# Score products for the GQA maxima: 72 rows of the array instead of 64

## The chip, the cores and the metric

The kernel runs on one core of a Trainium2 chip. The metric is device time in microseconds, the median of several runs. The core's engines each work through their own queue in order and wait for one another on semaphores: TensorE (PE, with its weight loads listed apart as PEld), VectorE (DVE), ScalarE (ACT), GpSimd (POOL), and SyncE (SP), which issues the weight stream's DMAs.

## The reference

One step of a two-layer backbone, float32. The 128 prompt tokens and 512 sample tokens go through the same layers; the sample's attention also reads a cache of 128 keys. Cut to what the change touches:

```python
def gqa_attend(q, k, v):                       # 8 query heads, 2 key heads, 64 features
    q5 = q.reshape(b, t, GQA_KV_HEADS, GQA_GROUP, HEAD_DIM)
    def blk(qb):
        s = jnp.einsum('bqkgd,bskd->bkgqs', qb, k).astype(jnp.float32) * scale
        p = jax.nn.softmax(s, axis=-1).astype(v.dtype)
        return jnp.einsum('bkgqs,bskd->bqkgd', p, v)
...
h = rms_norm(x, norm1_g) * (1 + sc1) + sh1
z = h @ w_in                                   # GQA q, k, v | gated convolution | differential q, k, v
... # per-head norms, rotary, o_g = gqa_attend, o_c = convolution, o_d = differential attention
x = x + g1 * (jnp.concatenate([o_g, o_c, o_d], axis=-1) @ w_out)
h = rms_norm(x, norm2_g) * (1 + sc2) + sh2
a, u = jnp.split(h @ ffn_up, 2, axis=-1)
x = x + g2 * ((jax.nn.silu(dwconv3(a, ffn_conv_w, ffn_conv_b)) * u) @ ffn_down)
```

The softmax of the sample runs over 640 keys (512 latent, 128 cached), that of the prompt over its own 128.

## The kernel before, in words

Tokens lie in five tiles of 128: tile 0 is the prompt, 1 to 4 the sample; the attention takes them in the order 1, 2, 3, 4, 0. Every large product is made in three passes of a reduced float32 type, from values split into a high and a low part: high by high, low by high, high by low. A layer runs through projections, attention, output projection and a gated MLP.

The part at issue is the GQA attention. Its operands stand with features on the partitions:

- `KG` holds a key head's high parts twice (rows 0 to 63 and 64 to 127), `KL` its low parts (rows 0 to 63) and ones in rows 64 to 71.
- `qTg` holds a tile's queries, high parts in rows 0 to 63 and low parts in 64 to 127; `qTm` holds the high parts again in rows 0 to 63, and in rows 64 to 71 the maxima that are to be taken off. Each has two places in turn (`s_q`, L1476), so a tile's queries are stacked, transposed on PE and evacuated while the tile before is at work (`q_tasks`, L1481; for the first two tiles `q_trans` and `q_evac`, L1341 and L1350).

First come scores with queries on the rows, made only for their maxima (`scores`, L1551). For each of the 8 heads `u` and each half of the keys (320 columns; 128 for the prompt) there are two products into one bank of the pair `p`:

```python
PE.matmul(o, q[:, u, :], KG[:, a_, c0:c0 + w], start=True, stop=False)
PE.matmul(o, q[0:64, u, :], KL[0:64, a_, c0:c0 + w], start=False, stop=True)
```

The queries are the weights. The first gives high by high and low by high over 128 rows, the second high by low over 64. DVE reduces the pair's 640 columns to one maximum (`maxima`, L1570). Four maxima are split, transposed on PE (`mm`) and written into rows 64 to 71 of `qTm` by DVE or ACT (`m_v`, `m_s`, L1604), each head's in its own row and zeros in the others. Then come the scores by key (`c_mm`, L1623), where keys are the weights: one product of KG with `qTg` over 128 rows and one of KL with `qTm` over 72 rows, whose ones add the negative maximum. ACT takes the exponential, PE multiplies by the values (`VG`, 64 weight columns), and POOL or DVE adds up the exponentials for the sums (`acc`). The differential attention beside it uses `KD` with 96 rows, into the same pairs `p`, and its exponentials `P` are transposed and multiplied by `VD`.

The order is set in two steps before anything runs. `Schedule` (L573) orders the attention's tasks by estimated times, places and a priority; a place such as one of `qTm`'s two (`Buf`) is free again when the stated number of readers has run. `Graph` (L181) then takes down every instruction with what it reads and writes, and emits them in the order of the best of 15 list plans made from estimated costs. All instructions bear the line of that helper, L316, in the profile, so they are told apart by their tiles.

Of the kernel before, what the change touches and what calls it, by code (L numbers as in the profile page):

```python
# [65 lines left out]
# us from the end of an instruction to the start of one that waits for it  # L66
# [8 lines left out]
class View:  # L75
    # A part of a tile that is made when its first instruction is emitted; `idx` holds the element numbers in a partition.
# [104 lines left out]
class Graph:  # L181
    # Takes down the instructions of the program in its order, with what each reads and writes, and emits them in an
    # order that keeps the engines busy: of the instructions whose inputs are there, the one that can wait least.
# [6 lines left out]
    # ---- pools and tiles  # L190
# [37 lines left out]
    def _places(self):  # L228
        # a tile's first instructions come after all of the tile's whose place it takes, and after its pool's opening
        for p in self.all:  # L230
            for n, row in p.tags.values():
                place = [None] * n
                for t in sorted((t for t in row if t.first is not None), key=lambda t: t.first.n):
                    i = min(range(n), key=lambda i: -1 if place[i] is None else place[i].ops[-1].n)
                    t.old, place[i] = place[i], t
                    t.kw = {**t.kw, "tag": f"{t.kw['tag']}_{i}", "bufs": 1}
        # pools that lie where closed ones lay come after them
        for p in self.pools:
            p.base = p.below.base + p.below.size if p.below else 0
            lo, hi = p.base, p.base + p.size  # L240
            if p.side == "right":
                top = SB_TOP if p.kind == "sb" else 16384
                lo, hi = top - hi, top - lo
            p.lo, p.hi = lo, hi
            p.under = [q for q in p.earlier if q.lo < hi and lo < q.hi]
            p.opened.before.update(q.shut for q in p.under)
        for p in self.all:
            for t in p.tiles:
                own = set(t.ops)
                for op in t.ops:  # L250
                    if op is t.first or not (op.deps & own):
                        op.before.add(p.opened)
                        if t.old is not None:
                            op.deps.update(t.old.ops)
                        for q in p.under:
                            op.deps.update(q.ops)
# [14 lines left out]
    # ---- instructions  # L271
# [58 lines left out]
    # ---- order  # L330
# [29 lines left out]
    def deadlines(self):  # L360
        """Priorities: the latest starts of the plan made from the end."""
# [5 lines left out]
        free = deque()  # L367
# [52 lines left out]
    def plan(self):  # L420
# [3 lines left out]
        later = {k: [] for k in now}       # (when the inputs are there, number, op)  # L424
        ready = {k: [] for k in now}       # (priority, number, when, op)
# [24 lines left out]
        while True:  # L450
# [24 lines left out]
            if op.extra:  # L475
                # bytes that the queues carry one after another
                e = self.queue(busy, now[k] + (2.6 if k == "G" else 1.2), op.extra) + 0.95
# [7 lines left out]
    def queue(self, busy, t, n):  # L485
        """Takes the first free time from t on among the busy ones (kept in order), returns its end."""
# [14 lines left out]
def cost(key, name, args, kw, outs, ins):  # L501
    """Estimated us on the engine, and on the DMA queues."""
# [37 lines left out]
class Slots:  # L540
    # interchangeable places; `free` holds when each can be taken again, None while it is held
    # with `line` the takers are served in order of urgency
# [9 lines left out]
class Buf:  # L552
    # a place held from the task that fills it to the last of `reads` readers
# [10 lines left out]
class Task:  # L564
    # alts: (engine, estimated us, emit); takes: buffers it fills first; reads: buffers it is done with
# [7 lines left out]
class Schedule:  # L573
    # Orders tasks for the engines' queues: whichever can start first, the more urgent one among near equals.
# [56 lines left out]
def tile_hybrid_prefix_dit_step(  # L631
# [38 lines left out]
    # banks b0..b3; beside them c0..c3, which the attention takes as the pairs p0 and p1  # L670
# [17 lines left out]
    def f32(t):  # L688
        return t.bitcast(F32)

# [5 lines left out]
    # sel[p, h] = 1 where p % 4 == h  # L696
    sel = T(P0, [128, 4], "sel")
    V.tensor_reduce(out=sel, in_=ident.rearrange("p (j h) -> p h j", h=4), axis=AX.X, op=ALU.add)
    # pick[:, r, q] = 1 where q == r
# [4 lines left out]
    # sum4[p, r] = 1 where p % 32 == r  # L704
# [19 lines left out]
    # silu(c) channel-major, zero-padded to 32 columns  # L724
# [8 lines left out]
    # vectors of a layer, channels on the partitions  # L733
# [87 lines left out]
    def mod_vec(l, v, k, raw):  # L821
        # the products of both conditions added up on DVE, then summed over the partitions
# [17 lines left out]
    def mod_quarter(q, v, g, raw):  # L840
        # the first two vectors in quarters of the channels; each 32 rows of the sums hold every fourth block of rows
# [55 lines left out]
    # order of the 128-row blocks of w_out: the convolution's first  # L897
# [114 lines left out]
    def tok_gemm(ah, al, nks, evac, tail=0, order=None, post=None, off=OFF, banks=ACC, tiles=range(NT)):  # L1012
        # the `tail` last units go tile by tile, the others block by block
# [35 lines left out]
    def chan_gemm(units, evacs, hh, hl):  # L1049
        # units: the banks of both halves of the columns; the first halves of all units come before the second ones  # L1050
# [11 lines left out]
    class Norm:  # L1062
# [8 lines left out]
        def sq(self, t, half):  # L1071
            # mean of squares of half the channels, with the guard in the first half's
# [34 lines left out]
        def mod(self, t, part, src=None):  # L1107
            # a quarter of the channels in place, or half of them from `src`
# [49 lines left out]
    def rope(z, t, H, d, key, tmp):  # L1158
        # z = z * cos * g + rot(z * g) * sin in place, [128, H, d]
# [14 lines left out]
    def rsqrt(ms):  # L1174
        # ms: [128, n] -> ms ** -0.5 in a new tile
# [17 lines left out]
    # ======================= layers =======================  # L1193
# [25 lines left out]
    for l in range(DEPTH):  # L1219
        a, b = (sides if l % 2 else sides[::-1])   # b: hT, mixa, attention, f; a: mixc, kv, prj, h2T  # L1220
# [22 lines left out]
        # keys, features on the partitions: [hi, hi]; [lo, ones that add a maximum]; [hi, lo, hi]  # L1243
# [6 lines left out]
        # key column / value tile index: sample tiles 0..3, cache 4, prompt 5  # L1250
# [18 lines left out]
        # ---- keys and queries: z views by kind  # L1269
# [32 lines left out]
        def split3(s, z, n, d, hi):  # L1302
            # z: [128, n, d] -> s: [128, n, 3, d], high parts at `hi`, the low part at the other place
# [37 lines left out]
        def q_trans(kind, t, half, bk):  # L1341
            # queries, features on the partitions: g [hi, lo], m [hi, maxima], d [hi, hi, lo]
            if half == 0:
                for tag in ("gm" if kind == "g" else "d"):
                    qT[tag, t] = T(kv, [128, 8, 128], f"qT{tag}{order.index(t)}", F32R)
            rows = 128 if kind == "g" else 96
# [12 lines left out]
        # ---- projections  # L1359
# [71 lines left out]
        # ---- gated short convolution  # L1431
# [24 lines left out]
        # ---- attention  # L1456
# [4 lines left out]
        # P transposed lies in buffers of the weight stream, which rest now  # L1461
# [6 lines left out]
        # GQA: first the scores by query, only for their maxima; then the scores by key with the maximum taken off  # L1468
        # in the product, their exponentials, the products with the values, and the sums by ones.
        # Differential: the scores by query, their exponentials, the pairs' difference, transposed for the values.  # L1470
# [10 lines left out]
        def q_tasks(i, t, kinds="dg"):  # L1481
            """Stacks and transposes the queries of tile t."""
            done, bufs = {}, {}
            for kind in kinds:
# [18 lines left out]
                for tag in tags:  # L1503
                    bufs[tag] = Buf(s_q[tag], {"g": 18, "m": 10, "d": 8}[tag] if t else {"g": 4, "m": 2, "d": 2}[tag])
                ends = []
                for half in range(2):
# [8 lines left out]
                    for tag in tags:  # L1515
                        r_ = {"g": 128, "m": 64, "d": 96}[tag]

                        def ev(e, bk=bk, tag=tag, half=half, r_=r_):
                            if half == 0:
                                # the second place for d is the first tile's used up row  # L1520
                                x = bufs[tag].tag == "qTd1"
                                qT[tag, t] = T(XQ if x else kv, [128, 8, 128], f"xq{order[0]}" if x else bufs[tag].tag, F32R)
                            o_ = qT[tag, t][0:r_, 4 * half:4 * half + 4, :]
# [9 lines left out]
        for i, t in enumerate(order[0:2]):  # L1533
            bufs = {}
            for tag in ("gmd" if i == 0 else "gm"):
                bufs[tag] = Buf(s_q[tag], {"g": 18, "m": 10, "d": 8}[tag])
# [4 lines left out]
        def attend(i, t):  # L1541
# [9 lines left out]
            def scores(gqa, us, sp):  # L1551
                def mm(o, u, c0, w):
                    if gqa:
                        q, a_ = qT["g", t], u // 4
                        PE.matmul(o, q[:, u, :], KG[:, a_, c0:c0 + w], start=True, stop=False)
                        PE.matmul(o, q[0:64, u, :], KL[0:64, a_, c0:c0 + w], start=False, stop=True)
# [19 lines left out]
            # ---- GQA  # L1576
            m_done, prev = [], None
            for a_ in range(2):
                nm_ = {}
                mx = None  # L1580
                for us in us_list[a_ * nS // 2:(a_ + 1) * nS // 2]:
# [3 lines left out]
                                takes=[sp], reads=[qb["g"]])  # L1585
# [129 lines left out]
            def spread(rb=rb, box=box):  # L1715
                # 1 / sum of every query and head to the head's 64 rows
# [10 lines left out]
            # ---- differential  # L1727
# [3 lines left out]
            for us in us_list:  # L1731
# [7 lines left out]
                for x, u in enumerate(us):  # L1739
# [11 lines left out]
                    if u % 2:  # L1751
                        rx = {}

                        def ratio(h=u // 2, rx=rx):
                            # lam * sum1 / sum2
# [119 lines left out]
        # ---- output projection + residual  # L1875
# [75 lines left out]
        # ---- gated MLP  # L1951
# [11 lines left out]
        for hf in range(2):  # L1963
# [25 lines left out]
            for mi in range(HB):  # L1989
                ev_a, ev_u = ahead or channels(mi)  # L1990
                if hf == mi == 0:
                    # the first columns of three products while the last tiles are normalized
# [101 lines left out]
```

## Time and profile before

| | |
|---|---|
| three runs | 1759.85, 1756.49 and 1762.54 us, median 1759.85 |
| profiled execution | span 1749.8 us, 24468 instructions; the page gives no other time of it |
| PE, PEld | 1720.8 us (98%), 1421.1 us (81%) |
| DVE, ACT, POOL | 1024.3 us (59%), 681.1 us (39%), 203.6 us (12%) |
| granted clock | 0.996 over the span |
| DMA | 171.53 MB, 98 GB/s on average |

The profile names an instruction by engine, operation and its tiles, as out<-in. A shape such as 64\*128 64x320 of a matmul is rows\*columns of the weights, and rows x columns of the operand that streams through. Matmuls overlap and their ends are modelled, so what one costs is read from its start to the next one's start. Of a timeline's row with xN, N equal instructions are merged into one.

### The profile page before, as it was taken

The numbers are of one execution on the slowest core, as the hardware profiler recorded it, in microseconds if no ns is written. First come the engines' busy times: TensorE is split into PE (matmuls) and PEld (weight loads), VectorE is DVE, ScalarE is ACT, GpSimd is POOL, SyncE is SP. The second block draws the span as 40 slices with busy tenths as digits, with TensorE's granted clock in tenths as the row PEclk, the third lists the DMA queues.
The fourth block names the chain that finished last, engine by engine and source line by source line (L and its number), as shares of the span: only waits on it lengthen the run. The fifth ranks groups of instructions, "written<-read, shape, count | busy, mean of one in ns | idle before, by whom it ended". The sixth has DMA issues, their size and how long they took to land.

```text
span 1749.8 us, 24468 instructions
## 1 busy us (share of the span) xinstructions
PE 1720.8 (98%) x9771; PEld 1421.1 (81%) x9771; DVE 1024.3 (59%) x1691; ACT 681.1 (39%) x1268; POOL 203.6 (12%) x298
## 2 busy tenths in 40 slices
PE   7999999999999999999999999999999999999998
PEld 4778655578999879999778895556899998899987
DVE  4757666656665767687446567665566643444423
ACT  5453456635332112232255526665452221123310
POOL 1321133211000000000022112332100000000000
PEclk9999999999999999999999999999999999999999
DMA  9543100053333544454333211002233322222212
GB/s 325 173 138 109 36 13 13 25 170 90 116 109 97 178 144 147 134 169 130 104 120 112 67 49 37 24 1 73 61 121 109 109 91 78 85 73 73 73 67 78
DMA packets 156542, 171.53 MB, mean 98 GB/s; under 512 B 6556, under 2 KB 121612, under 8 KB 155916
## 3 DMA queue, kind: packets, MB, share of 16 engines
q1 hardware_dynamic: 150940, 152.18, 28.0%
q0 software_dynamic: 5488, 17.79, 3.2%
q8 instruction: 77, 1.26, 0.3%
q14 instruction: 37, 0.30, 0.1%
HBM read 163.88 MB, written 6.06 MB: 97 GB/s over the span
## 4 chain that ended last, share of the span: by engine, by line
PE 93%; DVE 3%; ACT 2%; DMA 1%; issue 1%; POOL 0%; SPq 0%; ACTq 0%; DVEq 0%; POOLq 0%
PE c L316 47%; PE b L316 41%; PE p L316 6%; DMA raw<-in_w_mod_dram 1%; DVE xq L316 1%; ACT whi L316 1%; DVE sq L316 1%; DVE wlo L316 0%; ACT fu L316 0%; ACT xn L316 0%; DMA raw<-in_w_in_dram 0%; DVE qsg L316 0%; DVE macc L316 0%; ACT hh L316 0%; ACT junk L316 0%
## 5 line engine op out<-in xcount | busy, mean ns | idle before, releaser
L316 DVE TENSOR_TENSOR wlo<-raw,whi 128x1024 fp32r<-128x1024 f32 (+1 forms) x188 | 227.2, 1209 | 330.9 <-ACT whi L316 330.6
L316 PE MATMUL c<-hl,whi 128*128 128x322 f32 x1280 | 397.9, 311 | 1.1 <-DVE hl L316 1.1
L316 PE MATMUL c<-hh,whi 128*128 128x322 f32 x1280 | 398.5, 312 | 0.0
L316 PE MATMUL c<-hh,wlo 128*128 128x322 f32 x1280 | 397.3, 311 | 0.0
L316 ACT ACTIVATE whi<-raw 128x1024 fp32r<-128x1024 f32 (+1 forms) x188 | 195.4, 1041 | 507.8 <-PE b L316 284.2
L316 PEld LDWEIGHTS c<-hh,whi 128*128 128x128 f32 x1280 | 241.5, 189 | 2.6 <-issue 2.1
L316 PEld LDWEIGHTS c<-hl,whi 128*128 128x128 f32 x1280 | 241.2, 188 | 1.4 <-DVE hl L316 1.3
L316 PEld LDWEIGHTS c<-hh,wlo 128*128 128x128 f32 x1280 | 241.3, 189 | 0.0
L316 DVE TENSOR_REDUCE nmax<-p 128x1 f32<-128x640 f32 x128 | 104.2, 821 | 74.7 <-PE p L316 74.6
L316 DVE SCALAR_TENSOR_TENSOR macc<-raw,slc,macc 128x1024 f32<-128x1024 f32 x98 | 123.9, 1279 | 16.1 <-DMA raw<-in_w_mod_dram 15.7
L316 PE MATMUL b<-wlo,fh 128*128 128x512 f32 x264 | 104.3, 395 | 0.0
L316 PE MATMUL b<-whi,fh 128*128 128x512 f32 x264 | 104.2, 395 | 0.0
L316 PE MATMUL b<-whi,fl 128*128 128x512 f32 x264 | 104.1, 394 | 0.0
L316 PE MATMUL b<-hh,wlo 128*128 128x322 f32 x320 | 99.7, 311 | 0.0
L316 PE MATMUL b<-hh,whi 128*128 128x322 f32 x320 | 99.5, 311 | 0.0
L316 PE MATMUL b<-hl,whi 128*128 128x322 f32 x320 | 99.5, 311 | 0.0
L316 ACT ACTIVATE tv<-tv 128x644 f32<-128x644 f32 x44 | 32.6, 742 | 139.7 <-DVE tv L316 139.6
L316 DVE SCALAR_TENSOR_TENSOR tv<-asb,vec,tv 128x643 f32<-128x643 f32 x88 | 78.1, 887 | 2.3
L316 DVE TENSOR_TENSOR tv<-tv,c 128x322 f32<-128x322 f32 x88 | 42.6, 488 | 53.0 <-ACT tv L316 27.5
L316 PE MATMUL c<-whi,fh 128*128 128x512 f32 x176 | 69.6, 397 | 0.1
L316 PE MATMUL c<-wlo,fh 128*128 128x512 f32 x176 | 69.5, 395 | 0.0
L316 PE MATMUL c<-whi,fl 128*128 128x512 f32 x176 | 69.3, 394 | 0.0
(317 smaller groups left out, 3135.2 us busy)
## 6 DMA issues: line engine op xcount, KB each, us to landing
raw<-in_w_mod_dram SPq DMA_DIRECT2D x96, 512.0 KB, 4.2
raw<-in_ffn_up_dram SPq DMA_DIRECT2D x88, 512.0 KB, 4.5
raw<-in_ffn_down_dram SPq DMA_DIRECT2D x40, 512.0 KB, 3.6
raw<-in_w_in_dram SPq DMA_DIRECT2D x28, 512.0 KB, 4.8
raw<-in_w_in_dram SPq DMA_DIRECT2D x16, 256.0 KB, 4.7
raw<-in_w_out_dram SPq DMA_DIRECT2D x8, 512.0 KB, 3.5
raw<-in_w_out_dram SPq DMA_DIRECT2D x16, 256.0 KB, 4.0
gate<-gd POOLq DMA_DIRECT2D x4, 1024.0 KB, 5.8
```

What stands on the lines that cost most here:

```text
L316: getattr(real, name)(*a, **k)
```

## The change

The product of KL for the maxima takes its weights from `qTm` instead of `qTg`, and 72 rows instead of 64: the high parts of the queries, and the rows in which the maxima will stand, which are zero until then and meet the ones in KL. For this a memset on POOL zeroes rows 64 to 71 of every new `qTm` (8 partitions, 1024 values each). The readers counted for a place of `qTm` rise from 10 to 18 (from 2 to 4 for the prompt), and the score tasks are counted among them. All other lines of the diff only drop comments.

```diff
         def q_trans(kind, t, half, bk):
...
                     qT[tag, t] = T(kv, [128, 8, 128], f"qT{tag}{order.index(t)}", F32R)
+                    if tag == "m":
+                        G.memset(f32(qT[tag, t])[64:72], 0.0)
...
         def q_tasks(i, t, kinds="dg"):
...
-                    bufs[tag] = Buf(s_q[tag], {"g": 18, "m": 10, "d": 8}[tag] if t else {"g": 4, "m": 2, "d": 2}[tag])
+                    bufs[tag] = Buf(s_q[tag], {"g": 18, "m": 18, "d": 8}[tag] if t else {"g": 4, "m": 4, "d": 2}[tag])
...
                                 qT[tag, t] = T(XQ if x else kv, [128, 8, 128], f"xq{order[0]}" if x else bufs[tag].tag, F32R)
+                                if tag == "m":
+                                    G.memset(f32(qT[tag, t])[64:72], 0.0)
...
         for i, t in enumerate(order[0:2]):
...
-                bufs[tag] = Buf(s_q[tag], {"g": 18, "m": 10, "d": 8}[tag])
+                bufs[tag] = Buf(s_q[tag], {"g": 18, "m": 18, "d": 8}[tag])
...
             def scores(gqa, us, sp):
...
                         PE.matmul(o, q[:, u, :], KG[:, a_, c0:c0 + w], start=True, stop=False)
-                        PE.matmul(o, q[0:64, u, :], KL[0:64, a_, c0:c0 + w], start=False, stop=True)
+
+                        PE.matmul(o, qT["m", t][0:72, u, :], KL[0:72, a_, c0:c0 + w], start=False, stop=True)
...
                     s_ = sc.add([("PE", 0.54, lambda us=us, sp=sp: scores(True, us, sp))], qdone["g"] + [prev], p_,
-                                takes=[sp], reads=[qb["g"]])
+                                takes=[sp], reads=[qb["g"], qb["m"]])
```

On PE, in layer 0's attention, two heads of the second tile and what stands between them, before the change:

```order
L316 MATMUL p_435_2285<-KG_1255,qTg_310_2015 128x320
L316 MATMUL p_435_2285<-KL_814,qTg_310_2015 128x320
L316 MATMUL p_435_2285<-KG_1255,qTg_310_2015 128x320
L316 MATMUL p_435_2285<-KL_814,qTg_310_2015 128x320
L316 MATMUL b_405_2121<-wlo_2105,VG_831 64x512
L316 MATMUL p_439_2294<-KG_1255,qTg_310_2015 128x320
L316 MATMUL p_439_2294<-KL_814,qTg_310_2015 128x320
L316 MATMUL p_439_2294<-KG_1255,qTg_310_2015 128x320
L316 MATMUL p_439_2294<-KL_814,qTg_310_2015 128x320
L316 MATMUL b_446_2302<-ident_109,P_398_2118 128x128
```

The same place on PE with the change:

```order
L316 MATMUL p_435_2286<-KG_1259,qTg_310_2018 128x320
L316 MATMUL p_435_2286<-KL_814,qTm_311_854 128x320
L316 MATMUL p_435_2286<-KG_1259,qTg_310_2018 128x320
L316 MATMUL p_435_2286<-KL_814,qTm_311_854 128x320
L316 MATMUL b_405_2123<-wlo_2107,VG_842 64x512
L316 MATMUL p_439_2297<-KG_1259,qTg_310_2018 128x320
L316 MATMUL p_439_2297<-KL_814,qTm_311_854 128x320
L316 MATMUL p_439_2297<-KG_1259,qTg_310_2018 128x320
L316 MATMUL p_439_2297<-KL_814,qTm_311_854 128x320
L316 MATMUL b_446_2305<-ident_109,P_398_2120 128x128
```

Nothing moves: the KL products read `qTm` instead of `qTg`, and that is so through the attention of both layers. On PE only a few products of layer 0's projections change places.

On POOL, where the sums of the first tile's exponentials (`acc`) end, before:

```order
L316 TENSOR_TENSOR acc_408_2116<-acc_408_2116,wlo_2197 128x512 [waits Activation_49,Pool_49]
L316 TENSOR_TENSOR acc_416_2199<-acc_416_2199,wlo_2105 128x512 [waits Activation_49,Pool_49]
L316 TENSOR_TENSOR or_496_2272<-r_492_2226 128x4 [waits DVE_49]
L316 DMA xq_745_2377<-in_x_sample_dram 128x1024 [waits DMASW4_49,DVE_49]
L316 TENSOR_TENSOR acc_481_2479<-wlo_2197,wlo_2105 128x512 [waits Activation_49]
```

And with the change:

```order
L316 TENSOR_TENSOR acc_408_2118<-acc_408_2118,wlo_2199 128x512 [waits Activation_49,Pool_49]
L316 TENSOR_TENSOR acc_416_2201<-acc_416_2201,wlo_2107 128x512 [waits Activation_49,Pool_49]
L316 MEMSET qTm_437_2274 8x1024 [waits PE_49,Pool_49]
L316 TENSOR_TENSOR or_496_2288<-r_492_2228 128x4 [waits DVE_49,Pool_49]
L316 DMA xq_745_2380<-in_x_sample_dram 128x1024 [waits DMASW4_49,DVE_49]
```

The memset for the third tile's `qTm` (`qTm_437`) has come in behind the first tile's sums and ahead of the first step of its differential norm (`or`). The memsets of the fourth tile and of the prompt's stand at the same place one and two tiles later; those of the first two tiles stand ahead of the attention.

## Rows read from the trace of the kernel before

**Rows 1.** The page: its head, and the chain of waits by line.

```profile
span 1749.8 us, 24468 instructions
...
PE c L316 47%; PE b L316 41%; PE p L316 6%; DMA raw<-in_w_mod_dram 1%; DVE xq L316 1%; ACT whi L316 1%; DVE sq L316 1%; DVE wlo L316 0%; ACT fu L316 0%; ACT xn L316 0%; DMA raw<-in_w_in_dram 0%; DVE qsg L316 0%; DVE macc L316 0%; ACT hh L316 0%; ACT junk L316 0%
```

**Rows 2.** Window of layer 0's attention: length; busy PE, PEld, DVE, ACT, POOL; clock; DMA.

```profile
187.65:345.00 157.35, 156.77 (x782) 87.88 (x780) 103.51 (x186) 99.35 (x224) 46.84 (x49) 1.00 0.07 21
```

**Rows 3.** PE's groups by shape: count, busy us, mean ns, idle before.

```profile
L316 PE MATMUL p<-KL,qTg 64*128 64x320 f32 x128 | 52.3, 409 | 0.0
...
L316 PE MATMUL b<-KL,qTg 64*128 64x128 f32 x16 | 5.2, 323 | 0.0
```

**Rows 4.** Timeline of PE, 217 to 220 us: start, duration, instruction.

```profile
217.08 0.40 PE L316 MATMUL b<-qTm,KL 72*128 72x512 f32 x1
...
218.86 0.41 PE L316 MATMUL p<-KG,qTg 128*128 128x320 f32 x1
219.20 0.41 PE L316 MATMUL p<-KL,qTg 64*128 64x320 f32 x1
...
220.22 0.64 PE L316 MATMUL b<-ident,qsd 128*96 128x128 f32 x4
```

**Rows 5.** Timeline of PE's weight loads: the 64-row product at 219.20.

```profile
219.20 0.18 PEld L316 LDWEIGHTS p<-KL,qTg 64*128 64x128 f32 x1 [0.15 <-issue]
```

**Rows 6.** Timeline of PE, score products by key near 316 us.

```profile
316.08 0.40 PE L316 MATMUL b<-qTm,KL 72*128 72x512 f32 x1
316.31 0.40 PE L316 MATMUL b<-qTg,KG 128*128 128x512 f32 x1
```

**Rows 7.** Timeline of PE's weight loads there.

```profile
316.08 0.19 PEld L316 LDWEIGHTS b<-qTg,KG 128*128 128x128 f32 x1
```

**Rows 8.** Timeline of PE, two places with differential scores.

```profile
201.57 0.47 PE L316 MATMUL p<-KD,qTd 96*128 96x320 f32 x2
201.88 0.40 PE L316 MATMUL b<-qTm,KL 72*128 72x512 f32 x1
...
319.24 0.85 PE L316 MATMUL p<-KD,xq 96*128 96x320 f32 x4
320.02 0.64 PE L316 MATMUL b<-wlo,VG 128*64 128x512 f32 x1
```

**Rows 9.** Timeline of PE: eight transposes, and eight products of the prompt tile.

```profile
190.56 1.04 PE L316 MATMUL b<-ident,qsg 128*128 128x128 f32 x8
191.35 0.39 PE L316 MATMUL p<-KG,qTg 128*128 128x320 f32 x1
...
330.70 0.22 PE L316 MATMUL b<-KG,qTg 128*128 128x128 f32 x1
...
332.63 0.39 PE L316 MATMUL b<-ident,mm 128*8 128x128 f32 x2
```

**Rows 10.** Timeline of POOL: a memset of the kernel before.

```profile
68.59 1.38 POOL L316 MEMSET KL<- 8x1536 f32 x1
```

**Rows 11.** Timeline of ACT: the third tile's last evacuation into qTm.

```profile
231.85 0.59 ACT L316 ACTIVATE qTm<-b 64x512 fp32r<-64x512 f32 x1
```

**Rows 12.** Timeline of PE: the third tile's first head.

```profile
251.73 0.42 PE L316 MATMUL p<-KG,qTg 128*128 128x320 f32 x1
```

**Rows 13.** Instructions on tile p, DVE: count, min/median/max ns, first and last start.

```profile
L316 DVE TENSOR_REDUCE nmax<-p x128: 806/824/827, 189.1 to 1183.0; 128x1 f32<-128x640 f32 x128
```

**Rows 14.** Windows of 5 us in layer 0's attention, columns as in rows 2.

```profile
205.00:210.00 5.00, 4.42 (x16) 2.27 (x16) 4.64 (x10) 4.72 (x12) 2.06 (x2) 1.00 0.32 109
...
290.00:295.00 5.00, 5.00 (x21) 2.79 (x22) 4.98 (x8) 1.46 (x3) 4.32 (x4) 1.00 0.00 0
...
345.00:350.00 5.00, 5.00 (x19) 2.07 (x18) 2.71 (x10) 2.69 (x11) 0.55 (x3) 0.69 0.37 105
```

**Rows 15.** Timeline of PE, a score product by key with a late weight load.

```profile
206.21 0.50 PE L316 MATMUL b<-qTg,KG 128*128 128x512 f32 x1 [0.42 <-ACT qTm L316]
206.55 0.62 PE L316 MATMUL b<-qTm,KL 72*128 72x512 f32 x2
```

## The prediction, made before the changed kernel ran

> **What bounds the kernel now.** I read the chain of waits on the page first. It is TensorE nearly everywhere: PE has 93% of it, and the score products, which all go to tiles named p, have 6%, some 105 us of the 1749.8 us span [rows 1]. The change touches only the attention stage of each layer, so the next view is the table of busy time over that stage, 187.65 to 345.00 us in layer 0; layer 1 has the same stage once more. In 157.35 us PE is busy for 156.77, DVE for 103.51, ACT for 99.35 and POOL for 46.84 [rows 2]. So PE sets the pace there too, and the others have about a third of the stage free.
>
> The third view is PE's timeline, read from start to start, because the durations of matmuls overlap. One GQA head of a sample tile is four products of 320 columns: KG (128 rows), KL (64 rows), and the same two again for the other half of the keys. Each takes 0.34 us until the next one starts, and the head takes from 218.86 to 220.22, 1.36 us [rows 4]. The timeline of weight loads says why: the load of the 64-row product starts at 219.20, with its product and after 0.15 us in which no load ran [rows 5]. It does not run ahead across the border between 128 and 64 rows. The same stage holds the comparison. The later score products by key alternate a 128-row product from KG with a 72-row one from KL; they stream 512 columns, 1.6 times as many, and start 0.23 us apart [rows 6]. There the load for the product that starts at 316.31 begins at 316.08, while the product before it runs [rows 7]. A product of 72 rows thus follows and precedes one of 128 rows without the cost that 64 rows have. This is just what the change makes of the KL products for the maxima.
>
> **The change part by part.** *(a) Rows 64 to 72 in the head products.* The trace has 128 such products for the sample tiles, which makes 64 heads (8 heads, 4 tiles, 2 layers, two products each), and 16 for the prompt tile [rows 3]. What four products of 320 columns take without the border is shown by the differential scores, which have 96 rows: two of them in 0.31 us (201.57 to 201.88), so four in 0.62, and in another place four in 0.78 us (319.24 to 320.02), where a product with 64 weight columns follows [rows 8]. Heads are followed by either kind. I take 0.68, nearer the shorter row, since a head is as often followed by a wide product, such as the transpose of rows 4: 1.36 − 0.68 = 0.68 us a head, 64 × 0.68 = 43.5 us. The ends are 64 × 0.58 = 37 and 64 × 0.74 = 47 us.
>
> *(b) The prompt tile.* Eight products of 128 columns take 330.70 to 332.63, 0.24 us each; eight 128-column products without a border, the transposes at 190.56, take 0.79 us, 0.10 each [rows 9]. I take 0.12 saved on each of 32 products, 3.9 us; ends 0 and 4.5.
>
> The sum on PE is 47 us, between 37 and 52.
>
> [...]
>
> *(c) Zeros.* Ten memsets of 8 × 1024 are added on POOL, five a layer. The nearest row is the memset of 8 × 1536 at 1.38 us [rows 10], so I estimate 0.92 us each, 9.2 us of POOL. POOL has 110 us of a stage free. Three of the five stand behind the sums of exponentials of a tile and ahead of small steps of the differential norm. The one for the third tile follows the first tile's sums and waits for the old tile's last score product by key, at 217.08 [rows 4]. The tile's queries are evacuated until about 232.4 [rows 11] and its first head starts at 251.73 [rows 12], so the zeros have some 30 us. The head products now also wait for the evacuation into qTm, half a microsecond after that into qTg: the same 19 us of slack cover it. I cost these at nothing; if POOL's two memsets before the stage had no cover, they would cost 1.8 us a layer. The slot of qTm is held no longer than before, because its last reader was and is the product by key. In layer 0's projections a few products change places; PE has other work there.
>
> *(d) What is late next.* DVE reduces each head for 0.82 us [rows 13], so where heads follow one another almost bare, at the start of the stage, DVE paces them instead of PE at 0.68: 8 × 0.14 = 1.1 us a layer is not gained. Between the tiles a few heads fall where another engine is already full, as 290 to 295 us, with DVE busy 4.98 of 5 and POOL 4.32 [rows 14]. There a head's 0.68 can't come at once. With two heads at each of the three changes of sample tile, 4 us of a layer are lost if nothing is caught up. Over the stage DVE would be busy 103.5 of about 134 us, 77%, so most is caught up. I take 2.9 us for this and 1.1 for the first heads, 4 us a layer; ends 0 and 6.
>
> Off the path 8 of 47 us, then: 39 us gained. The span becomes 1749.8 − 39 = 1711. The page tells only the span of the profiled execution; the median of the runs shown is 1759.85, 10 us over it, and I carry that difference unchanged: 1759.85 − 39, rounded to **1720 us**. Its own range is 1759.85 − 52 = 1708 to 1759.85 − (37 − 12) = 1735.
>
> **The rivals.**
>
> *Other engines take over.* DVE, ACT and POOL run in order and wait for each other (scores, maximum, exponential, product), so 77% on average could be as full as they get. For it: the slice at 290 us, and 205 to 210, where DVE has 4.64 and ACT 4.72 of 5 and PE already idles for 0.58 [rows 14]. Against it: most heads lie elsewhere, and PE's order around them stays the same. If half of the gain went into new waits: 1759.85 − 24 = 1736 us.
>
> *Nothing changes.* Rows count for nothing on this array, a step is set by its columns, and the 0.34 us come from something else, such as the accumulation into the same bank. For it: the 128-row and the 64-row product of a head show the same duration, 0.41 us each [rows 4]. [...] Against it: the KG and KL pairs of rows 6 accumulate just so and step at 0.23. Time: 1760 us.
>
> *The loads stay exposed.* [...] The price is in a 72-row product at 206.55 that follows a KG product whose own load was late: that step is 0.34 us where 0.23 is usual, 0.11 more [rows 15]. A head would take 4 × (0.15 + 0.11) = 1.04 us, gaining 0.32: 64 × 0.32 = 20 us, and 1739 us.
>
> [...]
>
> **How the numbers follow.** Forecast 0.72, other engines 0.12, loads exposed 0.06, nothing 0.05, slower 0.05. The range 1706 to 1740 us takes in the forecast's own range and both partial gains. About 0.3%, 5 us, is what a measurement of this kernel can tell from no change: faster 0.90, within it 0.05, slower 0.05.
>
> **What would show it.** A head's four products start to start in 0.6 to 0.8 us, with the loads of KL beginning before their products; a stage of about 135 us with DVE at 77% of it; DVE's waits for p much shorter; POOL's new memsets without anyone waiting for them; the clock at 1.00 until the stage's end. Steps still at 0.34 us would refute (a); steps of 0.25 would speak for the exposed loads; short steps with PE idle for over 15 us a stage, for the engines.

## The result and the profile after

The change made the kernel faster, and by more than the forecast of 1720 us. The time lies 1 us inside the low end of the range of 1706 to 1740.

| | before | after |
|---|---|---|
| four runs of each, side by side | median 1758.17 us (1756.37 to 1762.54) | median 1707.14 us (1704.23 to 1709.54) |
| ratio, 95% interval | | 0.9713 [0.969, 0.9736] |
| profiled execution | span 1749.8 us | span 1704.3 us, time 1706.38 us |

The head of the page after and its chain of waits by line, to be held against [rows 1]:

```profile
span 1704.3 us, 24487 instructions
...
PE c L316 48%; PE b L316 41%; PE p L316 3%; DVE xq L316 1%; DVE sq L316 1%; ACT whi L316 1%; ACT xn L316 1%; DVE wlo L316 1%; ACT fu L316 0%; DMA raw<-in_w_mod_dram 0%; ACT junk L316 0%; DVE qsg L316 0%; DVE nmax L316 0%; DVE macc L316 0%; ACT hh L316 0%
```

Only one entry moves by more than a per cent: the score products, PE p, fall from 6% of the span to 3%. Layer 0's attention up to the same place in the program, as in [rows 2]:

```profile
185.65:321.00 135.35, 134.29 (x787) 83.90 (x784) 105.14 (x186) 99.79 (x226) 50.29 (x52) 1.00 0.08 24
```

It takes 135.35 us where it took 157.35. PE is still busy for all but 1.06 us of it; the other engines have the same work as before in less time, DVE 105.14 of 135.35, which is 78%. The groups of the KL products for the maxima, as in [rows 3]:

```profile
L316 PE MATMUL p<-KL,qTm 72*128 72x320 f32 x128 | 39.6, 315 | 0.0
...
L316 PE MATMUL b<-KL,qTm 72*128 72x128 f32 x16 | 3.8, 269 | 0.0
```

A head on PE's timeline, as in [rows 4], with the products ahead of it and behind it:

```profile
210.15 1.08 PE L316 MATMUL b<-wlo,VG 128*64 128x512 f32 x4
211.16 0.42 PE L316 MATMUL p<-KG,qTg 128*128 128x320 f32 x1
211.41 0.31 PE L316 MATMUL p<-KL,qTm 72*128 72x320 f32 x1
211.56 0.31 PE L316 MATMUL p<-KG,qTg 128*128 128x320 f32 x1
211.71 0.31 PE L316 MATMUL p<-KL,qTm 72*128 72x320 f32 x1
211.86 0.60 PE L316 MATMUL b<-ident,qsd 128*96 128x128 f32 x4
```

And the weight loads of that head, as in [rows 5]:

```profile
211.15 0.19 PEld L316 LDWEIGHTS p<-KG,qTg 128*128 128x128 f32 x1 [0.81 <-DVE nmax L316]
211.26 0.19 PEld L316 LDWEIGHTS p<-KL,qTm 72*128 72x128 f32 x1
211.41 0.19 PEld L316 LDWEIGHTS p<-KG,qTg 128*128 128x128 f32 x1
211.56 0.19 PEld L316 LDWEIGHTS p<-KL,qTm 72*128 72x128 f32 x1
```

The head lasts from 211.16 to 211.86, 0.70 us, against 1.36. Each load now starts 0.15 us before its own product, while the product before it streams. The one exception is the head's first load: it begins only with its product, and the step behind it is 0.25 instead of 0.15. The bracket names DVE, but the last release that this head waited for came at 210.71, 0.45 us before the load. What stands ahead of it is a product with 64 weight columns, and all 18 heads behind products with 64 or 8 weight columns have this late load and this 0.25. A differential product behind such a one shows the same, and the head behind that steps at 0.15 from its first product on:

```profile
208.14 0.42 PE L316 MATMUL p<-KD,qTd 96*128 96x320 f32 x1
208.39 0.31 PE L316 MATMUL p<-KG,qTg 128*128 128x320 f32 x1
208.54 0.31 PE L316 MATMUL p<-KL,qTm 72*128 72x320 f32 x1
```

Their weight loads:

```profile
208.14 0.19 PEld L316 LDWEIGHTS p<-KD,qTd 96*128 96x128 f32 x1 [0.81 <-ACT wlo L316]
208.25 0.19 PEld L316 LDWEIGHTS p<-KG,qTg 128*128 128x128 f32 x1
```

No run changes those narrow products, so this is read from the rows alone.

The sums of all of PE's steps, from one start to the next (a stage here reaches from the start of the first head to the start of the output projection's last product; both layers):

| us | before | after | difference |
|---|---|---|---|
| sample heads, 64 | 85.7 | 47.4 | −38.3 |
| prompt products, 32 | 7.6 | 3.6 | −3.9 |
| the rest of both stages | 356.4 | 354.6 | −1.9 |
| all else in the span | 1300.1 | 1298.7 | −1.4 |
| span | 1749.8 | 1704.3 | −45.5 |

### The profile page after: what moved, and what is told of

It is laid out like the page before. It is cut to its first block, busy times and chain, and to the rows that moved or that the text cites. A ratio compares the mean times of both kernels' runs of the same rounds, so it can differ in the third digit from the quotient of the medians.

```text
span 1704.3 us, 24487 instructions
## 1 busy us (share of the span) xinstructions
PE 1674.7 (98%) x9771; PEld 1411.9 (83%) x9771; DVE 1027.5 (60%) x1691; ACT 680.7 (40%) x1268; POOL 215.0 (13%) x308
## 4 chain that ended last, share of the span: by engine, by line
PE 92%; DVE 3%; ACT 3%; DMA 1%; issue 1%; POOL 0%; ACTq 0%; DVEq 0%; POOLq 0%
PE c L316 48%; PE b L316 41%; PE p L316 3%; DVE xq L316 1%; DVE sq L316 1%; ACT whi L316 1%; ACT xn L316 1%; DVE wlo L316 1%; ACT fu L316 0%; DMA raw<-in_w_mod_dram 0%; ACT junk L316 0%; DVE qsg L316 0%; DVE nmax L316 0%; DVE macc L316 0%; ACT hh L316 0%
```

## The experiments

Experiments 1 to 9 were each timed beside the kernel before, and what each edits is told against the changed kernel. They form three groups, each on a chip of its own: 1, 2, 3 and 5, then 4, 6, 7 and 8, then 9. The kernel before had medians of 1759.1, 1758.37 and 1756.61 us there, so 2 us between experiments of different groups tell nothing.

**1. All of the change but the rows.** The KL product takes 64 rows again; zeros, places and source of the weights stay.

```diff
-PE.matmul(o, qT["m", t][0:72, u, :], KL[0:72, a_, c0:c0 + w], start=False, stop=True)
+PE.matmul(o, qT["m", t][0:64, u, :], KL[0:64, a_, c0:c0 + w], start=False, stop=True)
```

> All of the change is kept (zeros, places, readers, the source qTm) except that the KL product of the heads uses rows 0 to 63 again. Theory (the border between 128-row and 64-row products costs about 0.2 us on each side): the heads are back at 1.36 us and the time at about 1758 us, the same as before. Rival (the gain came from another source tile, from the places or from the moved projections): about 1707 us, as with the change.

Measured: 1759.54 us, ratio 1.0013 [0.9986, 1.004]. The rows alone make the gain.

**2. One row past 64.** The same line with `0:65`, where the 65th row meets the zeros.

> The KL product of the heads uses 65 rows, the 64 of the queries and one row of zeros. Theory (what counts is whether the product still fits the half of the array, so one row past 64 is enough): as with the change, about 1707 us. Rival (the cost grows row by row with the difference to 128, or stops at some later row): between 1707 and 1758 us.

Measured: 1707.82 us, ratio 0.9708 [0.9675, 0.9741], the same as with 72 (1707.14), where 64 rows took 1759.54. One row past 64 takes off all that 72 rows take off; how many more are used made no difference.

**3. 64 rows in both products of a head.** KG's product loses its lower half as well, so that a head has no border inside it. The low part of the queries is left out of the maxima.

```diff
-PE.matmul(o, q[:, u, :], KG[:, a_, c0:c0 + w], start=True, stop=False)
+PE.matmul(o, q[0:64, u, :], KG[0:64, a_, c0:c0 + w], start=True, stop=False)
...
-PE.matmul(o, qT["m", t][0:72, u, :], KL[0:72, a_, c0:c0 + w], start=False, stop=True)
+PE.matmul(o, qT["m", t][0:64, u, :], KL[0:64, a_, c0:c0 + w], start=False, stop=True)
```

> Both products of a head use 64 rows; the low part of the queries is left out of the maxima. Theory (the border costs, not the 64 rows): within a head the steps are 0.15 us, and only the entry and the exit of a head pay 0.2 us each; a head takes about 1.0 instead of 1.36 us, 64 x 0.36 = 23 us, so about 1735 us. Rival (a 64-row product is slow by itself, its weights never load ahead): steps of 0.25 to 0.34 us, 1750 us or more. Rival (only the pair of different rows in one accumulation costs): 1707 us.

Measured: 1726.1 us, ratio 0.9819 [0.9782, 0.9856], 9 us below the 1735 that I expected. A head on PE's timeline in this kernel:

```profile
185.88 0.60 PE L316 MATMUL b<-ident,qsd 128*96 128x128 f32 x4
186.41 0.41 PE L316 MATMUL p<-KG,qTg 64*128 64x320 f32 x1
186.66 0.30 PE L316 MATMUL p<-KL,qTm 64*128 64x320 f32 x1
186.80 0.30 PE L316 MATMUL p<-KG,qTg 64*128 64x320 f32 x1
186.95 0.31 PE L316 MATMUL p<-KL,qTm 64*128 64x320 f32 x1
187.18 0.31 PE L316 MATMUL b<-ident,qsd 128*96 128x128 f32 x1
```

And its weight loads, with the idle time before them in brackets:

```profile
186.41 0.18 PEld L316 LDWEIGHTS p<-KG,qTg 64*128 64x128 f32 x1 [0.18 <-issue]
186.51 0.19 PEld L316 LDWEIGHTS p<-KL,qTm 64*128 64x128 f32 x1
186.66 0.18 PEld L316 LDWEIGHTS p<-KG,qTg 64*128 64x128 f32 x1
186.81 0.18 PEld L316 LDWEIGHTS p<-KL,qTm 64*128 64x128 f32 x1
187.18 0.12 PEld L316 LDWEIGHTS b<-ident,qsd 128*96 128x96 f32 x1 [0.19 <-issue]
```

Among themselves 64-row products step at 0.14 to 0.15 us and their loads run ahead, so the rows as such cost nothing. The cost sits where a head begins and ends, that is, where PE crosses between 64-row and taller products: the load of the product behind the border does not run ahead, the last step before it is 0.23 instead of 0.15, and the first one behind it 0.25. A crossing thus costs 0.08 to 0.09 us in the step before it and 0.10 of a load that nothing covers, 0.19 together (0.34 − 0.15). The head of [rows 4] had four crossings: four longer steps, three uncovered loads inside it, and the late first load that it keeps after the change, 0.60 + 4 × 0.09 + 3 × 0.10 + 0.10 = 1.36 us. The fourth uncovered load falls on the product behind it.

The 9 us below 1735 are, by an estimate from the same steps, crossings that cost nothing extra. In the changed kernel the first step is 0.25 behind narrow products (18 heads) and the last one 0.24 ahead of products with 64 or 32 weight columns (20 heads), with no border at 64 rows. Of the 128 crossings 38 thus add nothing, some 7 us; the prompt tile, 7.6 us before and 4.4 here, gives 3 more.

**4. The zeros five times.** Each memset is issued five times.

```diff
-G.memset(f32(qT[tag, t])[64:72], 0.0)
+[G.memset(f32(qT[tag, t])[64:72], 0.0) for _ in range(5)]
```

> The change, with each of its ten memsets issued five times: 40 more at 0.95 us, 38 us more work on POOL. Theory (the zeros lie beside other work, with some 20 us or more to spare): 1707 us, within 3. Rival (they are on the path, or hold up the sums and norms behind them on POOL): up to 38 us more; if only what stands ahead of the attention counts, about 2 x 7.6 us more, 1722 us.

Measured: 1706.08 us, ratio 0.97 [0.9681, 0.9719]. Some 38 us more of POOL cost nothing.

**5. No KL product for the maxima.** Product and memsets are left out, and the places are counted as before the change; the planner then chooses another order. The maxima lack the low part of the keys, which shifts the exponents only.

```diff
-PE.matmul(o, q[:, u, :], KG[:, a_, c0:c0 + w], start=True, stop=False)
+PE.matmul(o, q[:, u, :], KG[:, a_, c0:c0 + w], start=True, stop=True)
...
-PE.matmul(o, qT["m", t][0:72, u, :], KL[0:72, a_, c0:c0 + w], start=False, stop=True)
+pass
```

> The KL product is left out of the maxima altogether, and the memsets with it: the scores for the maxima lack high by low of the keys; the maxima only shift the exponents of the softmax. Theory (PE still sets the pace of the attention after the change): the KL steps of the changed kernel, 23.1 us for the sample and 2.1 us for the prompt, go, about 1682 us. Rival (DVE, with 0.82 us a head against 0.35 us on PE, and ACT take over): half of it, about 1695 us, or nothing, 1707 us, with PE idle for over 15 us a stage.

Measured: 1704.87 us, ratio 0.9694 [0.9662, 0.9725]. Hardly better than the change, though 25.1 us of PE steps are gone. Either another engine had become the bound, or the other order lost it.

**6. Half the reduction.** The changed kernel in its order, but the maximum of the sample heads is taken over the second 320 keys only: 64 reductions of some 0.47 us instead of 0.82. The cost that the planner reckons with stays, so the order does too; the differential calls, not shown, keep all keys.

```diff
-            def maxima(us, sp, nm_):
+            def maxima(us, sp, nm_, gqa=True):
...
-                V.tensor_reduce(out=nm_["t"][:, us[0] % 4:us[0] % 4 + len(us)], in_=view(sp),
-                                axis=AX.XY if smp else AX.X, op=ALU.max, negate=True)
+                V.tensor_reduce(out=nm_["t"][:, us[0] % 4:us[0] % 4 + len(us)],
+                                in_=sp.t[:, 1, 0:320] if smp and gqa else view(sp),
+                                axis=AX.XY if smp and not gqa else AX.X, op=ALU.max, negate=True)
+                if smp:
+                    graph.ops[-1].dur = 0.069 + 640 / 960
...
```

> The change in the same order, but the maximum of a sample head is taken over the second half of its keys alone (320 instead of 640 columns; it only shifts the exponents): DVE does about 64 x 0.35 = 22 us less. Theory (PE still sets the pace after the change): 1707 us, within 3. Rival (DVE is as much the bound by now): 1695 us or below.

Measured: 1702.25 us, ratio 0.9686 [0.9668, 0.9704]. Of 22 us taken off DVE 4.9 came back (3.8 against experiment 4 of the same group). So in the changed kernel the length of these reductions holds PE up for at most some 5 us.

**7. Both: no KL product, half the reduction**, in the order of experiment 5.

> No KL product for the maxima, and the maximum of a sample head over half of the keys, in the order of the kernel without the KL product (1704.9 us). Theory (without the KL product DVE sets the pace, 0.82 us a head against about 0.35 on PE): DVE's 22 us come off in good part, 1690 us or below. Rival (the latency from engine to engine or ACT): 1702 us or more.

Measured: 1700.29 us, ratio 0.9672 [0.965, 0.9694], 4.6 us less than without the half reduction. The length of the reductions isn't what held experiment 5 either.

**8. No KL product, in the change's own order.** Only the instruction is not issued, so that the maxima lack the same part as in experiment 5; zeros, places and plan stay.

```diff
-                        PE.matmul(o, q[:, u, :], KG[:, a_, c0:c0 + w], start=True, stop=False)
+                        PE.matmul(o, q[:, u, :], KG[:, a_, c0:c0 + w], start=True, stop=True)

                         PE.matmul(o, qT["m", t][0:72, u, :], KL[0:72, a_, c0:c0 + w], start=False, stop=True)
+                        graph.ops[-1].emit = lambda: None
```

> The change in exactly its own order, with the KL product for the maxima left out and the zeros kept: 25 us less on PE. The kernel without it gained only 2.3 us, but its order differed too. Theory (another engine takes over): again about 1704 us, PE idle or stretched by waits. Rival (the other order ate the gain): 1682 us.

Measured: 1693.67 us (1693.15 to 1693.91), ratio 0.9633 [0.9618, 0.9648]. This beats both kernels, and some 11 us of the loss in experiment 5 was its order. Two heads on PE's timeline:

```profile
211.75 0.56 PE L316 MATMUL p<-KG,qTg 128*128 128x320 f32 x2
212.15 0.60 PE L316 MATMUL b<-ident,qsd 128*96 128x128 f32 x4
212.59 0.60 PE L316 MATMUL b<-ident,qsg 128*128 128x128 f32 x4
213.29 0.56 PE L316 MATMUL p<-KG,qTg 128*128 128x320 f32 x2
213.78 1.07 PE L316 MATMUL b<-whi,VG 128*64 128x512 f32 x2
```

Two products take 0.40 or 0.49 us rather than 0.30, since the head's longer steps, the first (late load, 0.25) and the last where products with 64 weight columns follow (0.24), are now two of two and not two of four. At four places of a layer the head products also wait longer, for DVE or ACT; the longest is at 189 us, where one pair p is still being reduced and the step is 1.22 us. KG's head steps grow from 24.3 to 31.7 us, about half by each of the two. The rest of the stages grows by some 4 us, and of 25.1 us 13.6 are left in the stages.

**9. As 8, with half the reduction.**

> The changed kernel in exactly its order, with the KL products for the maxima of all heads not issued (zeros and places kept), and the sample heads' maximum taken over the second half of their keys only, which is some 22 us less of DVE. Theory A (with the KL products gone PE's gain is partly held by DVE, which reduces a head in 0.82 us while PE makes it in about 0.45): of the 11.5 us that went to waits in the kernel without the KL products, most come back: about 1684 us. Rival B (the waits are those of the chain from maxima over mm and qTm to the scores by key, whose latency does not depend on the length of one reduction, or are with ACT): 1690 to 1694 us, within 4 us of the kernel without the KL products.

Measured: 1691.25 us (1690.09 to 1692.2), ratio 0.9626 [0.959, 0.9662]. The 2.4 us less are within what the two ratios leave open, as the rival said: what experiment 8 left in the stages, 25.1 − 13.6 = 11.5 us, does not come back with shorter reductions. PE still waits for DVE and ACT at the same places. The step that waits for a pair is shorter, 0.60 us where it was 1.22, but one just behind it, which waits for DVE's split of the differential queries (tile qsd), is longer, 1.33 where it was 0.49.

**10. The kernel before once more**, for its clock.

> The kernel before once more, for its granted clock. Theory (the clock falls in many of its executions among the GQA heads of the attention, where 64-row products leave PE's array without columns for most of a step): this execution's time is 1750 to 1770 us and its mean granted clock .985 to .997; if it is above 1756 us, its trace shows a stretch at half clock in one of the two attention stages, between the first head and the last. Rival (the spread between executions of the kernel before has nothing to do with the heads): the clock is at 1.00 throughout both stages up to their ends, whatever the time.

Measured: 1760.4 us, span 1758.6, mean granted clock 0.990. Three windows of layer 0's attention, columns as in [rows 2]; the clock is the third figure from the end:

```profile
187.91:194.80 6.89, 6.89 (x31) 4.24 (x28) 4.26 (x7) 4.45 (x8) 0.02 (x1) 1.00 0.00 0
194.80:211.90 17.10, 17.10 (x39) 8.81 (x40) 8.33 (x15) 5.67 (x13) 2.37 (x3) 0.50 0.10 32
211.90:346.00 134.10, 133.54 (x655) 73.88 (x654) 87.19 (x155) 84.13 (x188) 44.43 (x47) 1.00 0.07 20
```

A head inside the middle one:

```profile
197.15 0.61 PE L316 MATMUL p<-KG,qTg 128*128 128x320 f32 x1
197.70 0.63 PE L316 MATMUL p<-KL,qTg 64*128 64x320 f32 x1
198.26 0.63 PE L316 MATMUL p<-KG,qTg 128*128 128x320 f32 x1
198.82 0.63 PE L316 MATMUL p<-KL,qTg 64*128 64x320 f32 x1
199.39 0.88 PE L316 MATMUL b<-ident,qsd 128*96 128x128 f32 x3
```

For 17.1 us, among the first heads, the granted clock is 0.50 instead of 1.00, and a step of a head takes 0.56 us instead of 0.34. Layer 0's stage, by the sums above, is 236.8 us where it was 228.2 in the profiled execution, and that is nearly all of the difference of the spans (8.8 us). Experiment 1, which has the same heads, shows the same:

```profile
195.00:212.00 17.00, 17.00 (x40) 8.79 (x39) 7.58 (x14) 6.35 (x16) 1.83 (x2) 0.50 0.13 34
```

The profiled execution of before, in which I had read 1.00 over the whole stage, was one of its fastest: with the 1.8 us by which time and span differ here, it took some 1751.6 us.

## Why the prediction was right, step by step

*The bound.* Right: PE paced the stage before and still does.

*(a) The head products.* The cause was right; experiments 1 to 3 show it to be the border at 64 rows (1759.54 us with 64 rows in the KL product, 1707.82 with 65, 1726.1 with 64 in both products). Predicted 43.5 us, measured 38.3: a head takes 47.4 / 64 = 0.74 us in the mean and not 0.68, and before it took 1.34 and not 1.36. The bare head is as forecast (0.60 at its shortest, 0.70 in the rows above). What I had not counted is the head's first step. It is 0.15 us in 8 heads only, which follow wide products; behind transposes it is 0.23 (36 heads), behind products with 64 or 8 weight columns 0.25 (18 heads), and 0.25 in two heads that wait for DVE. Over the 64 heads that is 4.9 us more than 0.15 each.

*(b) The prompt tile.* Predicted 3.9 us (32 × 0.12 is 3.8), measured 3.9. Four of its products on the timeline, 0.11 us each in the mean against the 0.24 of [rows 9]:

```profile
307.22 0.22 PE L316 MATMUL b<-KG,qTg 128*128 128x128 f32 x1
307.28 0.28 PE L316 MATMUL b<-KL,qTm 72*128 72x128 f32 x1
307.39 0.27 PE L316 MATMUL b<-KG,qTg 128*128 128x128 f32 x1
307.50 0.28 PE L316 MATMUL b<-KL,qTm 72*128 72x128 f32 x1
```

*(c) The zeros.* Right, and by experiment 4 with much room. On POOL's timeline the memset stands where the order had it, and lasts 0.95 us, where I estimated 0.92:

```profile
212.39 0.95 POOL L316 MEMSET qTm<- 8x1024 f32 x1
213.41 0.20 POOL L316 TENSOR_TENSOR or<-r 128x4 f32<-128x4 f32 x1
```

*(d) What is late next.* Mis-sized, and the term that was furthest off: I took 8 us off for heads that DVE paces. Outside the heads nothing was lost: the rest of the stages got 1.9 us shorter. Inside them PE waits for a reduction at one head of each layer, where the step is 0.63 instead of 0.15, about 1 us in all:

```profile
189.06 0.31 PE L316 MATMUL p<-KL,qTm 72*128 72x320 f32 x1
189.69 0.41 PE L316 MATMUL p<-KG,qTg 128*128 128x320 f32 x1 [0.31 <-DVE nmax L316]
```

Experiment 6 bounds what the length of the reductions costs at some 5 us. The two terms (a) and (d) together were 35.5 us predicted, 40.2 measured. That (a) was 5 us too generous and (d) 10 us too cautious, so that half of the error cancels, is luck. Full slices like those of [rows 14] are still there, at other places. From the first head to 205 us PE idles for 1.06 us, which is all of its idle time in this stage; later it has no gap, even where DVE and POOL are both full:

```profile
190.00:195.00 5.00, 4.83 (x31) 3.93 (x30) 4.99 (x9) 2.90 (x9) 0.57 (x1) 1.00 0.31 108
275.00:280.00 5.00, 5.00 (x30) 3.12 (x27) 4.87 (x7) 2.52 (x5) 4.92 (x4) 1.00 0.00 0
```

What DVE gave up is waiting. Its idle time until PE's tile p was there, in us and times, over the whole program before:

```profile
  PE p L316: 74.6, 84
```

and after:

```profile
  PE p L316: 33.8, 52
```

*The 10 us from span to median.* This step failed too. I carried the difference between the profiled span (1749.8) and the median (1759.85) over as if it were fixed. About 2 us of it are: after, the profiled time is 1706.38 for a span of 1704.3. The other 8 are the spread between executions of before, and it goes with the clock: of the thirteen beside experiments 1, 2, 3 and 5, one at a mean of 0.996 took 1750.83 us and one at 0.985 took 1765.01. Experiment 10 shows for one execution where the clock falls, among the heads; for the others that is not shown. After, the profiled time is 0.8 us under the median and the four runs have mean clocks of 0.995 to 0.997, where the seven of before in experiment 9's comparison have 0.989 to 0.997. So the span fell by 45.5 us where I had 39, and the medians by 51.0, so that the time lies 1 us below the 1708 that the sum itself allowed.

*The rivals.* Other engines did not take half: 45.5 us of span against 47 on PE. The loads do not stay exposed: but for a head's first one they start 0.15 us ahead, and 128- and 72-row loads run ahead of one another (the load at 211.26 for the product at 211.41, that at 211.41 for the one at 211.56). That nothing changes fell with the steps at 0.15. Nor did it get slower: after, the clock is at 1.00 from 185.65 to 321 us and from 1008 to 1165, over the heads of both layers. It fell among the heads of 64 rows instead, to 0.50 in experiments 1 and 10, where I had read 1.00 from one execution.

What lowers the clock among those heads stays open. Experiment 3, with 64 rows throughout and one crossing at each end of a head, shows it too (the level is 0.50 from 1037.6 to 1047.9 us, among layer 1's heads; mean clocks 0.988 to 0.994). Ahead of the two stretches of 17 us PE had not been idle since the first head (in experiment 10 it was busy for 6.89 of 6.89 us); ahead of that of experiment 3 it was busy for 7.27 of 7.60. Experiments 5 and 7, which have no 64-row product, have mean clocks of 0.992 to 0.997; where in those executions the clock fell is not shown. With 72 rows the two stages after stand at 1.00, as above, and with 65 rows experiment 2 has 1.00 in every window of layer 0's heads; the mean clocks of the profiled executions of 2, 4 and 6 are 0.997, 0.997 and 0.999. No run separates the rows from the crossings here.

## What to carry to other kernels

Look at the steps between starts where products of 64 rows alternate with taller ones, and at the loads there: if the load begins with its product, padding past 64 rows with zeros can cost less than the crossing; here the steps went from 0.34 to 0.15 us, and the zeros cost nothing that experiment 4 could show. Look at the first step behind products with few weight columns too: here it was 0.25 instead of 0.15 with 72 rows as well. Before a span is carried to a median, compare the profiled execution's own time with all runs, and take the difference for clock until another profiled execution of the same kernel says otherwise; here it was some 8 of 10 us. When an instruction is taken out to price it, keep the order; here a new plan hid 11 us (1704.87 against 1693.67).

## What was not expected

- A crossing between 64-row and taller products cost 0.19 us on PE (0.34 − 0.15), in two about equal parts (a longer step before it, an uncovered load behind it), while the rows by themselves cost nothing (64-row products among themselves stepped at 0.14 to 0.15 us, 72- and 128-row ones at 0.15); 65 rows did as well as 72 (1707.82 and 1707.14 us).
- TensorE, busy by the profile for all of it, had a granted clock of 0.50 for 17 us in two of the three profiled executions of kernels with such heads (17.1 us in experiment 10, 17.0 in experiment 1, not in the first profile of before). Busy in the profile was no sign of a full clock.
- Leaving out the low part of the keys from the maxima altogether is worth another 13.5 us (experiment 8 against the change's 1707.14), in a place where the products had seemed necessary.
